# Five plain transposes for both halves of a value column, and partition sums in three column tiles

## The chip, the cores and the metric

The kernel runs on one core of one Trainium2 chip. The metric is the device time of one execution in microseconds (us); lower is better. TensorE (PE) multiplies; its weight loads are listed apart as PEld. VectorE (DVE), ScalarE (ACT) and GpSimd (POOL) do elementwise work, and SyncE (SP) issues nearly all DMAs, in order, from one queue.

## The reference

Two layers of a decoder trunk on 512 prompt tokens and 64 sample tokens (8 sequences of 8), all in float32:

```
h = x + 0.5 * rmsnorm(swiglu(rmsnorm(x)))            # ff1: 1024 -> 2816 -> 1024
z = rmsnorm(h) @ w_in                                # 3584 columns: aq|ak|av|bq|bf|bi|bg
a = dilated window attention(aq, ak, av)             # 8 heads of 64; the samples also read 2048 cached rows
b = HGRN2(q=silu(bq), f=lb+(1-lb)*sigmoid(bf), i=bi) # 4 heads of 128, chunkwise recurrence
b = rmsnorm(b) * silu(bg)
h = h + rmsnorm([rmsnorm(a), b] @ w_out)
h = h + 0.5 * rmsnorm(swiglu(rmsnorm(h)))            # ff2
```

It returns the trunk's output, the new keys and values of both groups of tokens, and the HGRN2 states.

## The kernel before, in words

Tokens lie along the free dimension. They are cut into two halves (hf 0 and 1) of 288: 256 prompt tokens and 32 sample tokens each. Features lie on the 128 partitions. Every weight tile of 128 rows by 128 columns is split into a high and a low part (L114 on ACT, L116 on DVE), and each product is three matmuls (L357 to L359) of 128x288. PE's rows of these three lines are called products below; 24 of them make one output column block of one half.

A layer runs ff1, the input projection with both mixers beside it (`mixing`), w_out, and ff2. In `mixing`, column block i runs for half 0 and then for half 1. Blocks 0 to 7 are queries and keys, blocks 8 to 11 the attention values, blocks 12 to 23 the HGRN2 columns of four heads (every third of them a value column), 24 to 27 the gates. Between products the kernel pulls steps of side work: the samples' attention (`sample`: scores `sc` L860, transposes of the weights `ptps` L895, weighted sums `pov` L915), the prompt's attention (`psc`, `ptp`, `ppv`) and the HGRN2 heads (`lev`, `kv`, `po`). A scheduler in the tile framework then sets the final order on each engine from the program and from its own estimate of times.

Three pieces matter here.

- `tok_major` (L505 to L512) turns a value column to token-major form. For each half it makes two plain transposes of 128 tokens (L508), and for the 32 samples a matmul with the identity (L509) that sits in one 32-column tile of the array (`tile_position=(0, 32*hf)`). Two ACT copies move the result out of PSUM. There are 8 value columns in a layer, so 16 halves. The evacuated column `z` (L525) comes from a ring of six shared temporaries, and for blocks 8 to 11 a DMA per half writes it to `o_v` (L532).
- `stats` (L200 to L217) sums squares over the partitions: three matmuls `stat` (L204) with 96 tokens as stationary columns and a column of ones moving. DVE (L206) and POOL (L207) make the inverse root, and three transposes `bc` (L212) spread it over the partitions. A float32 matmul that is not a transpose appears in the trace as two passes, so the 3 appear as 6.
- `kv_load` (L817 to L830) streams the cached keys and values in tiles of 256 KB through a ring of KVB = 9 buffers. The load into a buffer waits until PE has used the tile that was there; it stands in SP's one queue with the weight loads and the writes.

The PSUM tiles of the products (`mm`) in blocks 4 to 27 come from a pool of two: a new block may start only when the block two before it has been evacuated.

Of the kernel before, what the change touches and what calls it, by code (L numbers as in the profile page):

```python
# [19 lines left out]
P = 128  # L20
D = 1024
NJ = 8
NF = 22
CHUNKS = ((0, 8), (8, 15), (15, 22))
H = 288
HP = 256
# [5 lines left out]
XBUF = 5  # L32
ZBUF = 2
ABUF = 2
KVB = 9
G_OFF = {}
_o = 0
for _n, _w in (("ff1_pre_g", 8), ("ff1_post_g", 8), ("mix_pre_g", 8), ("attn_norm_g", 4), ("hgrn_norm_g", 1),
# [9 lines left out]
def trunk_step(ctx: ExitStack, tc: tile.TileContext, a, L):  # L48
    nc = tc.nc

    pe, act, dve, pool, sp = nc.tensor, nc.scalar, nc.vector, nc.gpsimd, nc.sync
# [4 lines left out]
    cp = ctx.enter_context(tc.tile_pool(name="consts", bufs=1))  # L56
# [85 lines left out]
    logit = const("logits", [P, L, 4])  # L142
    ones = cp.tile([P, 1], F32, name="ones")
    dve.memset(ones[:], 1.0)
    warm = cp.tile([P, 1], F32, name="warm")
# [14 lines left out]
    lbm = cp.tile([P, 4], F32, name="lbm")  # L160
    lbe = cp.tile([P, L, 4], F32, name="lbe")
    lbs = cp.tile([P, 4], F32, name="lbs")
# [4 lines left out]
    def late_consts():  # L167
        lstage = tmp("lstage")[:, :NLM * 32].rearrange("p (a b) -> p a b", b=32)
        for n, t in (("logits", logit), ("lmask", lstage), ("pbias", pbias), ("sb_str", sb_str), ("sb_rec", sb_rec),
                     ("sb_new", sb_new), ("bmask", bmask), ("eye32", eye32), ("sel", sel)):  # L170
            sp.dma_start(t if n == "lmask" else t[:], a[n])
        dve.tensor_copy(lmask[:], lstage)

        dve.tensor_copy(lbm[:], logit[:, 0, :])
        for l in range(1, L):
            dve.tensor_tensor(lbm[:], lbm[:], logit[:, l, :], op=ALU.max)
        for l in range(L):
            dve.tensor_tensor(lbe[:, l, :], logit[:, l, :], lbm[:], op=ALU.subtract)
        act.activation(lbe[:], lbe[:], AF.Exp)
        dve.tensor_copy(lbs[:], lbe[:, 0, :])  # L180
        for l in range(1, L):
            dve.tensor_tensor(lbs[:], lbs[:], lbe[:, l, :], op=ALU.add)
        dve.reciprocal(lbs[:], lbs[:])
        for l in range(L):
            dve.tensor_tensor(lbe[:, l, :], lbe[:, l, :], lbs[:], op=ALU.mult)
        dve.tensor_copy(lbm[:], lbe[:, 0, :])
        for l in range(L):
            if l:
                dve.tensor_tensor(lbm[:], lbm[:], lbe[:, l, :], op=ALU.add)
            dve.tensor_tensor(fof[:, l, :], lbm[:], lbe[:, 0, :], op=ALU.subtract)  # L190
            dve.tensor_scalar(fsc[:, l, :], fof[:, l, :], -0.5, 0.5, op0=ALU.mult, op1=ALU.add)
            dve.tensor_scalar(nfs[:, l, :], fsc[:, l, :], -1.0, None, op0=ALU.mult)
            dve.tensor_tensor(fof[:, l, :], fof[:, l, :], fsc[:, l, :], op=ALU.add)


    def tmp(name="tmp"):
        return tp.tile([P, H], F32, name=name, tag="tmp", bufs=6)


    def stats(acc, inv, out_psum=False, tag="rb"):  # L200

        s = ps_hg.tile([P, 512], F32, name="stat", tag="hg")
        for c in range(3):
            pe.matmul(s[:96, c:c + 1], acc[:, 96 * c:96 * c + 96], ones[:, 0:1], start=True, stop=True)  # L204
        sm = tp.tile([96, 4], F32, name="sm", tag="sm", bufs=2)
        dve.tensor_scalar(sm[:, :3], s[:96, :3], inv, EPS, op0=ALU.mult, op1=ALU.add)  # L206
        pool.tensor_tensor(sm[:, :3], sm[:, :3], nhalf[:96, :3], op=ALU.pow)  # L207
        yield
        yield
        b = ps_hg.tile([P, 512], F32, name="bc", tag="hg")  # L210
        for c in range(3):
            pe.transpose(b[:, 96 * c:96 * c + 96], sm[:, c:c + 1].to_broadcast([96, P]), ident[:96, :96])  # L212
        if out_psum:
            return b[:, :H]
# [122 lines left out]
    late = []  # L337
# [134 lines left out]
    def mixing(l, chains, xpool_close, x_spill):  # L472
        o = [None, None]
        with ExitStack() as es:
# [7 lines left out]
            z = {}  # L482
# [19 lines left out]
                    z[name, h] = pools["hp"].tile([P, 2, H], F32, name=name, bufs=ZBUF)  # L502
                return z[name, h]

            def tok_major(src, hf, dst, dst_s, cols):  # L505
                ps = ps_pr.tile([P, 512], F32, name="tr", tag="pr")
                for q in range(2):
                    pe.transpose(ps[:, q * P:(q + 1) * P], src[:, q * P:(q + 1) * P], ident[:])  # L508
                pe.matmul(ps[32 * hf:32 * hf + 32, 2 * P:3 * P], src[:, HP:H], ident[:], start=True, stop=True,  # L509
                          tile_position=(0, 32 * hf))  # L510
                act.activation(dst[:, 2 * hf:2 * hf + 2, cols], ps[:, :HP].rearrange("p (a b) -> p a b", a=2), AF.Copy)
                act.activation(dst_s[32 * hf:32 * hf + 32, cols], ps[32 * hf:32 * hf + 32, 2 * P:3 * P], AF.Copy)  # L512

            def evac(i, hf, pst):
                ps = pst[:, :H]
                r = rn[hf]
                if i < 8:
                    dst = (aq if i < 4 else ak)[:, i % 4, hf, :]
                    dve.tensor_tensor(dst, ps, r, op=ALU.mult)
                    if i == 7 and hf == 1:  # L520
                        late.append(lambda: sp.dma_start(a["o_k"][l], ak[:]))
                    return
                t = tmp("z")
                if i < 12 or (i < 24 and i % 3 == 2):
                    dve.tensor_tensor(t[:], ps, r, op=ALU.mult)  # L525
                else:
                    dve.scalar_tensor_tensor(t[:], ps, 0.5, r, op0=ALU.mult, op1=ALU.mult)
                    th = tmp("th")
                    act.activation(th[:], t[:], AF.Tanh)
                if i < 12:  # L530
                    m = i - 8
                    sp.dma_start(a["o_v"][l, :, m, hf, :], t[:])  # L532
                    late.append(lambda: tok_major(t, hf, vt, vts, slice(m * P, (m + 1) * P)))
                    return
                h, kind = divmod(i - 12, 3) if i < 24 else (i - 24, 3)
                if hf == 0 and kind < 3 and h >= 2:
                    while stage[h - 2] < kind + 1:
                        drain()
                if kind == 0:
                    dve.tensor_scalar(zt("zf", h)[:, hf, :], th[:], fsc[:, l, h:h + 1], fof[:, l, h:h + 1],  # L540
                                      op0=ALU.mult, op1=ALU.add)
                    pool.tensor_scalar(zt("zk", h)[:, hf, :], th[:], nfs[:, l, h:h + 1], fsc[:, l, h:h + 1],
                                       op0=ALU.mult, op1=ALU.add)
                elif kind == 1:
                    dve.scalar_tensor_tensor(zt("zq", h)[:, hf, :], th[:], 1.0, t[:], op0=ALU.add, op1=ALU.mult)
                elif kind == 2:
                    if ("vh", h) not in z:
                        z["vh", h] = pools["hp"].tile([P, 4, P], F32, name="vh", bufs=ZBUF)
                        z["vhs", h] = pools["hp"].tile([64, P], F32, name="vhs", bufs=ZBUF)
                    late.append(lambda: tok_major(t, hf, z["vh", h], z["vhs", h], slice(0, P)))  # L550
# [636 lines left out]


def _outs(L):
    return {"o_y": (2, P, NJ, H), "o_k": (L, P, 4, 2, H), "o_v": (L, P, 4, 2, H), "o_sp": (L, 4, P, P),  # L1190
            "o_ss": (L, 4, P, NB, P)}


def _unpack(r, L):
    y = np.transpose(r["o_y"], (0, 3, 2, 1)).reshape(2, H, D)
    yp = np.ascontiguousarray(y[:, :HP]).reshape(1, 2 * HP, D)
    ys = np.ascontiguousarray(y[:, HP:]).reshape(NB, 8, D)

    def kv(t):
        t = np.transpose(t, (0, 3, 4, 2, 1)).reshape(L, 2, H, 8, 64)  # L1200
        return (np.ascontiguousarray(t[:, :, :HP]).reshape(L, 1, 2 * HP, 8, 64),
                np.ascontiguousarray(t[:, :, HP:]).reshape(L, NB, 8, 8, 64))

    kp, ks = kv(r["o_k"])
    vp, vs = kv(r["o_v"])
# [22 lines left out]
```

## Time and profile before

| what | value |
|---|---|
| median of 3 runs | 2571.57 us (2571.02 to 2574.45) |
| the profiled execution | 2571.23 us, of which the span from first to last instruction 2569.4 us |
| PE busy | 2523.4 us, 98% of the span |
| DVE, ACT, POOL busy | 1183.7, 903.5, 380.4 us |
| granted clock | 0.997 of full speed |

PE is busy nearly all of the time. Its matmuls are pipelined: the trace gives each a duration of some 0.29 us, but the next one starts about 0.13 us later. What a piece of side work costs is therefore read from starts: how much later the next products start than they would have.

### The profile page before, as it was taken

The page shows a single profiled execution, that of the slowest core. Times are in us where ns is not written, and L with a number is a line of the kernel's source. Part 1 is how long each engine was busy: PE and PEld are TensorE (multiplying, and loading weights), DVE is VectorE, ACT ScalarE, POOL GpSimd, SP SyncE. Part 2 cuts the span into 40 slices and gives each one's busy share as a digit, 9 for nine tenths or more (in the row PEclk, how much of TensorE's full clock was granted, in tenths as well). Part 3 has the DMA queues.
Part 4 walks back from the last instruction along what each step waited for, and adds up shares of the span by engine and source line. Part 5 has one row for each costly group of instructions (what it writes and reads, how often), then busy time and mean ns, then how long its engine had stood idle before and what let it go on. Part 6 is the DMA issues. An engine that isn't in the chain of part 4 may idle for free.

```text
span 2569.4 us, 52156 instructions
## 1 busy us (share of the span) xinstructions
PE 2523.4 (98%) x21876; PEld 2384.3 (93%) x21876; DVE 1183.7 (46%) x2648; ACT 903.5 (35%) x2031; POOL 380.4 (15%) x450
## 2 busy tenths in 40 slices
PE   8999999999999999999999999999999999999997
PEld 8999999877778999999999999998777799999997
DVE  6324335435655742433463334362456557323343
ACT  5222235133335532222542222351333354322232
POOL 1101012002312210101220010120022122101013
PEclk9999999999999999999999999999999999999999
DMA  5222222475543322222222222235754442222221
GB/s 173 83 84 81 91 76 92 169 255 176 187 166 109 100 83 84 82 89 78 88 75 83 83 82 88 77 104 182 253 198 151 155 131 81 86 85 75 91 76 45
DMA packets 108747, 292.04 MB, mean 114 GB/s; under 512 B 12896, under 2 KB 16224, under 8 KB 107744
## 3 DMA queue, kind: packets, MB, share of 16 engines
q1 hardware_dynamic: 108080, 288.29, 34.9%
q8 instruction: 172, 2.82, 0.5%
q14 instruction: 63, 0.52, 0.1%
q10 hardware_dynamic: 432, 0.41, 0.0%
HBM read 272.14 MB, written 16.52 MB: 112 GB/s over the span
## 4 chain that ended last, share of the span: by engine, by line
PE 91%; DVE 4%; issue 2%; POOL 1%; ACT 1%; DMA 0%; SPq 0%; POOLq 0%; ACTq 0%; DVEq 0%
PE gu L358 14%; PE gu L359 14%; PE gu L357 14%; PE mm L357 12%; PE mm L358 12%; PE mm L359 12%; PE sc L860 2%; PE pov L915 1%; PE ppv L800 1%; PE psc L776 1%; POOL sm L207 1%; PE stat L204 1%; PE ptp L791 1%; DVE y L317 1%; PE wo L358 1%
## 5 line engine op out<-in xcount | busy, mean ns | idle before, releaser
L357 PE MATMUL gu<-xh,whi 128*128 128x288 f32 x2752 | 811.6, 295 | 7.4 <-ACT xh L271 6.5
L358 PE MATMUL gu<-xl,whi 128*128 128x288 f32 x2752 | 813.4, 296 | 0.3
L359 PE MATMUL gu<-xh,wlo 128*128 128x288 f32 x2752 | 811.6, 295 | 0.0
L114 ACT ACTIVATE whi<-wraw 128x512 fp32r<-128x512 f32 (+1 forms) x688 | 395.0, 615 | 723.2 <-PE gu L358 357.3
L116 DVE TENSOR_TENSOR wlo<-wraw,whi 128x512 fp32r<-128x512 f32 (+1 forms) x688 | 445.9, 680 | 206.6 <-ACT whi L114 188.6
L357 PEld LDWEIGHTS gu<-xh,whi 128*128 128x128 f32 x2752 | 518.4, 188 | 8.7 <-ACT xh L271 6.9
L358 PEld LDWEIGHTS gu<-xl,whi 128*128 128x128 f32 x2752 | 518.4, 188 | 1.6 <-DVE xl L272 1.6
L359 PEld LDWEIGHTS gu<-xh,wlo 128*128 128x128 f32 x2752 | 518.5, 188 | 0.0
L358 PE MATMUL mm<-hl,whi 128*128 128x288 f32 x1408 | 415.6, 295 | 0.0
L357 PE MATMUL mm<-hh,whi 128*128 128x288 f32 x1408 | 415.0, 295 | 0.0
L359 PE MATMUL mm<-hh,wlo 128*128 128x288 f32 x1408 | 414.6, 294 | 0.0
L438 POOL TENSOR_TENSOR gate<-gate,rb 128x288 f32<-128x288 f32 x176 | 162.9, 925 | 1261.9 <-ACT gate L437 1261.9
L357 PE MATMUL mm<-xh,whi 128*128 128x288 f32 x1088 | 333.9, 307 | 0.7 <-DVE y L453 0.7
L358 PE MATMUL mm<-xl,whi 128*128 128x288 f32 x1088 | 325.7, 299 | 0.0
L359 PE MATMUL mm<-xh,wlo 128*128 128x288 f32 x1088 | 325.0, 299 | 0.0
L359 PEld LDWEIGHTS mm<-hh,wlo 128*128 128x128 f32 x1408 | 264.7, 188 | 0.0
L357 PEld LDWEIGHTS mm<-hh,whi 128*128 128x128 f32 x1408 | 264.6, 188 | 0.0
L358 PEld LDWEIGHTS mm<-hl,whi 128*128 128x128 f32 x1408 | 264.4, 188 | 0.0
L442 DVE TENSOR_TENSOR hid<-gu,gate 128x288 f32<-128x288 f32 x172 | 78.7, 457 | 329.2 <-PE gu L359 320.9
L357 PEld LDWEIGHTS mm<-xh,whi 128*128 128x128 f32 x1088 | 204.4, 188 | 21.1 <-issue 17.6
L358 PEld LDWEIGHTS mm<-xl,whi 128*128 128x128 f32 x1088 | 204.9, 188 | 10.0 <-issue 9.1
L359 PEld LDWEIGHTS mm<-xh,wlo 128*128 128x128 f32 x1088 | 204.9, 188 | 6.8 <-issue 6.6
(196 smaller groups left out, 2373.3 us busy)
## 6 DMA issues: line engine op xcount, KB each, us to landing
wraw<-in_wgu SPq DMA_DIRECT2D x175, 512.0 KB, 3.5
kv<-in_kc SPq DMA_DIRECT2D x160, 256.0 KB, 4.1
kv<-in_vc SPq DMA_DIRECT2D x160, 256.0 KB, 3.9
wraw<-in_wd SPq DMA_DIRECT2D x64, 448.0 KB, 3.3
wraw<-in_w_in SPq DMA_DIRECT2D x56, 512.0 KB, 4.2
wraw<-in_wd SPq DMA_DIRECT2D x32, 512.0 KB, 3.5
wraw<-in_w_out SPq DMA_DIRECT2D x16, 512.0 KB, 4.2
xs<-x SPq DMA_DIRECT2D x4, 1152.0 KB, 4.4
```

Source lines behind the costliest of these rows:

```text
L114: act.activation(whi[i][:, c], r[:, c], AF.Copy)
L116: dve.tensor_tensor(wlo[i][:, c], r[:, c], f(whi[i][:, c]), op=ALU.subtract)
L204: pe.matmul(s[:96, c:c + 1], acc[:, 96 * c:96 * c + 96], ones[:, 0:1], start=True, stop=True)
L207: pool.tensor_tensor(sm[:, :3], sm[:, :3], nhalf[:96, :3], op=ALU.pow)
L317: ins = dve.tensor_tensor(y[:, js, :], y[:, js, :], rb[:, None, :].to_broadcast([P, 2, H]), op=ALU.mult)
L357: pe.matmul(ps, wh[:, s], xhi[:, j, :], start=(n == 0), stop=False)
L358: pe.matmul(ps, wh[:, s], xlo[:, j, :], start=False, stop=False)
L359: pe.matmul(ps, wl[:, s], xhi[:, j, :], start=False, stop=(n == k - 1))
L438: pool.tensor_tensor(g[:], g[:], rn[hf], op=ALU.mult)
L442: dve.tensor_tensor(h[:], ps, gate[hf][:], op=ALU.mult)
L776: pe.matmul(dst, q, kk, start=True, stop=True, tile_position=(64 * s, 0))
L860: pe.matmul(ps[32 * p:32 * p + 32, c], qbd[:, 2 * bp + bb, p, :], rhs(p), start=(bb == 0), stop=(bb == 1), tile_position=(0, 32 * p))
```

## The change

`tok_major` now runs once for a value column, when both halves are evacuated into one tile `zt` of 576 columns. Half 1 is stored with its samples next to those of half 0 (two DVE operations in place of one), so that the turn is four plain transposes of 128 tokens and a fifth of 64 tokens, into two PSUM tiles, with two ACT copies. `zt` has one buffer. The write of `o_v` is one DMA for both halves, and the host puts the columns back in order. `stats` makes nine matmuls of 32 stationary columns, one in each of three column tiles for each of three token groups, in place of three of 96. KVB falls from 9 to 8. The constants behind the lower bounds (`logits` and what is worked out of them) move into a temporary tile.

```
-KVB = 9
+KVB = 8
...
         s = ps_hg.tile([P, 512], F32, name="stat", tag="hg")
         for c in range(3):
-            pe.matmul(s[:96, c:c + 1], acc[:, 96 * c:96 * c + 96], ones[:, 0:1], start=True, stop=True)
+            for q in range(3):
+                pe.matmul(s[32 * q:32 * q + 32, c:c + 1], acc[:, 96 * c + 32 * q:96 * c + 32 * q + 32], ones[:, 0:1],
+                          start=True, stop=True, tile_position=(0, 32 * q))
...
-            def tok_major(src, hf, dst, dst_s, cols):
+            def tok_major(src, dst, dst_s, cols):
                 ps = ps_pr.tile([P, 512], F32, name="tr", tag="pr")
-                for q in range(2):
-                    pe.transpose(ps[:, q * P:(q + 1) * P], src[:, q * P:(q + 1) * P], ident[:])
-                pe.matmul(ps[32 * hf:32 * hf + 32, 2 * P:3 * P], src[:, HP:H], ident[:], start=True, stop=True,
-                          tile_position=(0, 32 * hf))
-                act.activation(dst[:, 2 * hf:2 * hf + 2, cols], ps[:, :HP].rearrange("p (a b) -> p a b", a=2), AF.Copy)
-                act.activation(dst_s[32 * hf:32 * hf + 32, cols], ps[32 * hf:32 * hf + 32, 2 * P:3 * P], AF.Copy)
+                for c in range(4):
+                    o_ = c * P + 64 * (c // 2)
+                    pe.transpose(ps[:, c * P:(c + 1) * P], src[:, o_:o_ + P], ident[:])
+                pn = ps_pr.tile([P, 512], F32, name="trs", tag="pr")
+                pe.transpose(pn[:64, :P], src[:, HP:HP + 64], ident[:])
+                act.activation(dst[:, :, cols], ps[:].rearrange("p (a b) -> p a b", a=4), AF.Copy)
+                act.activation(dst_s[:, cols], pn[:64, :P], AF.Copy)
...
-                t = tmp("z")
                 if i < 12 or (i < 24 and i % 3 == 2):
-                    dve.tensor_tensor(t[:], ps, r, op=ALU.mult)
+                    if hf == 0:
+                        z["t"] = qp.tile([P, 2 * H], F32, name="zt")
+                    t2 = z["t"]
+                    if hf == 0:
+                        dve.tensor_tensor(t2[:, :H], ps, r, op=ALU.mult)
+                    else:
+                        dve.tensor_tensor(t2[:, H + 32:], ps[:, :HP], r[:, :HP], op=ALU.mult)
+                        dve.tensor_tensor(t2[:, H:H + 32], ps[:, HP:], r[:, HP:], op=ALU.mult)
...
-                    sp.dma_start(a["o_v"][l, :, m, hf, :], t[:])
-                    late.append(lambda: tok_major(t, hf, vt, vts, slice(m * P, (m + 1) * P)))
+                    if hf:
+                        sp.dma_start(a["o_v"][l, :, m], t2[:])
+                        late.append(lambda: tok_major(t2, vt, vts, slice(m * P, (m + 1) * P)))
```

The scheduler moves instructions on every engine. Three places show what the prediction speaks of. The first is on PE, in `mixing` of layer 0, where a sum (`stat`) of an HGRN2 head stands between the samples' `pov` and the next head's `lev`, both of which are in 32-column tiles. Before:

```order
L359 MATMUL mm<-xh_4545,wlo 128x288
L915 MATMUL pov<-kv,pts 32x128 x16
L204 MATMUL stat<-ones,osq 96x1 x3
L594 MATMUL lev<-zq,zk 32x32 x16
L791 MATMUL ptp<-ident,S 128x128 x7
L594 MATMUL lev<-zq,zk 32x32 x16
```

and now:

```order
L361 MATMUL mm<-xh_4560,wlo 128x288
L927 MATMUL pov<-kv,pts 32x128 x16
L205 MATMUL stat<-ones,osq 32x1 x9
L606 MATMUL lev<-zq,zk 32x32 x16
L803 MATMUL ptp<-ident,S 128x128 x4
L606 MATMUL lev<-zq,zk 32x32 x8
```

The sum keeps its place, but it is in column tiles like its neighbours.

The second is on PE at the attention values of layer 0, around the transposes `ptps` and the first sums `pov` of the samples. Before, products stand between `ptps` and `pov`, and the turn of one half (`tr`) lies around `pov`:

```order
L895 MATMUL ptps<-ident,ss 128x128 x2
L895 MATMUL ptps<-ident,ss 64x128
L357 MATMUL mm<-xh_4545,whi 128x288
L358 MATMUL mm<-xl_4546,whi 128x288
L359 MATMUL mm<-xh_4545,wlo 128x288
L508 MATMUL tr<-ident,z 128x128
L915 MATMUL pov<-kv,pts 32x128 x36
L508 MATMUL tr<-ident,z 128x128
L509 MATMUL tr<-ident,z 32x128
L357 MATMUL mm<-xh_4735,whi 128x288
```

Now `ptps` and `pov` follow each other at once, at the boundary between two blocks:

```order
L361 MATMUL mm<-xh_4756,wlo 128x288
L907 MATMUL ptps<-ident,ss 128x128 x10
L907 MATMUL ptps<-ident,ss 64x128
L927 MATMUL pov<-kv,pts 32x128 x32
L359 MATMUL mm<-xh_4560,whi 128x288
```

No product is left between them, and the turn of a whole value column stands one block later, in five plain transposes (`tr` x4 and `trs`):

```order
L360 MATMUL mm<-xl_4757,whi 128x288
L361 MATMUL mm<-xh_4756,wlo 128x288
L511 MATMUL tr<-ident,zt 128x128 x4
L513 MATMUL trs<-ident,zt 64x128
L927 MATMUL pov<-kv,pts 32x128 x4
```

The third is SP's queue from the end of the keys to the third attention value of layer 0; `kv` are the cache loads, `out_o_v` the writes of the values. Before:

```order
L521 DMA out_o_k<-ak 128x2304
L532 DMA out_o_v<-z 128x288
L826 DMA kv<-in_kc 128x512 x14
L532 DMA out_o_v<-z 128x288
L826 DMA kv<-in_kc 128x512 x6
L829 DMA kv<-in_vc 128x512 x2
L532 DMA out_o_v<-z 128x288
L829 DMA kv<-in_vc 128x512 x6
```

and now:

```order
L524 DMA out_o_k<-ak 128x2304
L838 DMA kv<-in_kc 128x512 x13
L543 DMA out_o_v<-zt 128x576
L838 DMA kv<-in_kc 128x512 x7
L841 DMA kv<-in_vc 128x512 x7
L543 DMA out_o_v<-zt 128x576
L841 DMA kv<-in_vc 128x512
```

The write of a whole column now stands behind 13 and then 14 cache loads, and the next evacuation into `zt` waits for that write.

## Rows read from the trace of the kernel before

**Rows 1.** The page: the chain that ended last, by engine
```profile
PE 91%; DVE 4%; issue 2%; POOL 1%; ACT 1%; DMA 0%; SPq 0%; POOLq 0%; ACTq 0%; DVEq 0%
```
**Rows 2.** Busy us by stretch: window, length, PE, PEld, DVE, ACT, POOL; clock, DMA, GB/s
```profile
496.60:546.90 50.30, 50.30 (x447) 34.58 (x447) 13.27 (x43) 13.96 (x36) 1.76 (x5) 1.00 0.78 252
546.90:805.80 258.90, 249.22 (x3231) 198.83 (x3231) 148.26 (x467) 97.19 (x275) 56.77 (x80) 0.99 0.53 177
```
**Rows 3.** Timeline of PE (start, us, line): one half's turn between products
```profile
495.82 0.29 PE L359 MATMUL mm<-xh,wlo 128*128 128x288 f32 x1
495.95 0.38 PE L508 MATMUL tr<-ident,z 128*128 128x128 f32 x2
496.26 0.41 PE L509 MATMUL tr<-ident,z 128*32 128x128 f32 x2
...
496.83 0.29 PE L358 MATMUL mm<-xl,whi 128*128 128x288 f32 x1
```
**Rows 4.** Timeline of PE: eight plain transposes between products
```profile
528.92 0.29 PE L359 MATMUL mm<-xh,wlo 128*128 128x288 f32 x1
529.06 1.04 PE L895 MATMUL ptps<-ident,ss 128*128 128x128 f32 x8
...
530.07 0.29 PE L358 MATMUL mm<-xl,whi 128*128 128x288 f32 x1
```
**Rows 5.** Timeline of PE: one sum of six 96-column passes between products
```profile
446.37 0.29 PE L359 MATMUL mm<-xh,wlo 128*128 128x288 f32 x1
446.51 0.59 PE L204 MATMUL stat<-ones,y 128*96 128x1 f32 x6
446.96 0.38 PE L357 MATMUL mm<-xh,whi 128*128 128x288 f32 x1
447.17 0.29 PE L358 MATMUL mm<-xl,whi 128*128 128x288 f32 x1
```
**Rows 6.** Timeline of PE: 32-column passes in four column tiles, in and out
```profile
586.65 0.29 PE L357 MATMUL mm<-xh,whi 128*128 128x288 f32 x1
586.88 0.46 PE L594 MATMUL lev<-zq,zk 128*32 128x32 f32 x32
587.15 0.26 PE L598 MATMUL lev<-zq,zk 128*32 128x32 f32 x4
...
594.09 0.26 PE L598 MATMUL lev<-zq,zk 128*32 128x32 f32 x4
594.27 0.40 PE L357 MATMUL mm<-xh,whi 128*128 128x288 f32 x1
594.51 0.29 PE L358 MATMUL mm<-xl,whi 128*128 128x288 f32 x1
```
**Rows 7.** Timeline of PE: a sum between two runs in column tiles
```profile
701.01 0.67 PE L204 MATMUL stat<-ones,osq 128*96 128x1 f32 x6
701.61 0.46 PE L594 MATMUL lev<-zq,zk 128*32 128x32 f32 x32
```
**Rows 8.** Timeline of DVE: second halves of the first and second value evacuated
```profile
496.14 0.46 DVE L525 TENSOR_TENSOR z<-mm,rb 128x288 f32<-128x288 f32 x1 [2.71 <-PE mm L359]
...
510.02 0.46 DVE L525 TENSOR_TENSOR z<-mm,rb 128x288 f32<-128x288 f32 x1 [0.28 <-PE mm L359]
```
**Rows 9.** Timeline of SP: the cache loads, and the write behind them
```profile
496.14 9.52 SPq L826 DMA_DIRECT2D kv<-in_kc  x14
505.75 0.38 SPq L532 DMA_DIRECT2D out_o_v<-z  x1
```
**Rows 10.** DMA issues: median us from issue to landing, the values' writes
```profile
out_o_v<-z SPq DMA_DIRECT2D x16, 144.0 KB, 3.9
```
**Rows 11.** Timeline of PE, then ACT: the last `ptps`, and its last copy
```profile
530.35 0.55 PE L895 MATMUL ptps<-ident,ss 128*128 128x128 f32 x3
...
531.21 0.26 ACT L903 ACTIVATE pts<-ptps 64x128 f32<-64x128 f32 x1
```
**Rows 12.** Groups by shape: weight loads of `pov`, idle before them
```profile
L915 PEld LDWEIGHTS pov<-kv,pts 128*32 128x32 f32 x1280 | 32.9, 109 | 6.6 <-issue 5.8 <-PE mm L358 0.4 <-DMA kv<-in_vc 0.2
```

More of the change, by code (lines that the diff above doesn't have):

```diff
@@ L141, in trunk_step @@
     sel = const("sel", [P, 32])
-    logit = const("logits", [P, L, 4])
     ones = cp.tile([P, 1], F32, name="ones")
@@ L158, in trunk_step @@
             dve.tensor_scalar(g_of(l, n), g_of(l, n), 0.5, None, op0=ALU.mult)
-    lbm = cp.tile([P, 4], F32, name="lbm")
-    lbe = cp.tile([P, L, 4], F32, name="lbe")
-    lbs = cp.tile([P, 4], F32, name="lbs")
     fsc = cp.tile([P, L, 4], F32, name="fsc")
@@ L167, in late_consts @@
     def late_consts():
+        lb = tmp("lb")
+        logit = lb[:, :4 * L].rearrange("p (a b) -> p a b", b=4)
+        lbe = lb[:, 4 * L:8 * L].rearrange("p (a b) -> p a b", b=4)
+        lbm, lbs = lb[:, 8 * L:8 * L + 4], lb[:, 8 * L + 4:8 * L + 8]
         lstage = tmp("lstage")[:, :NLM * 32].rearrange("p (a b) -> p a b", b=32)
@@ L170, in late_consts @@
                      ("sb_new", sb_new), ("bmask", bmask), ("eye32", eye32), ("sel", sel)):
-            sp.dma_start(t if n == "lmask" else t[:], a[n])
+            sp.dma_start(t if n in ("lmask", "logits") else t[:], a[n])
         dve.tensor_copy(lmask[:], lstage)
-        dve.tensor_copy(lbm[:], logit[:, 0, :])
+        dve.tensor_copy(lbm, logit[:, 0, :])
         for l in range(1, L):
-            dve.tensor_tensor(lbm[:], lbm[:], logit[:, l, :], op=ALU.max)
+            dve.tensor_tensor(lbm, lbm, logit[:, l, :], op=ALU.max)
         for l in range(L):
-            dve.tensor_tensor(lbe[:, l, :], logit[:, l, :], lbm[:], op=ALU.subtract)
-        act.activation(lbe[:], lbe[:], AF.Exp)
-        dve.tensor_copy(lbs[:], lbe[:, 0, :])
+            dve.tensor_tensor(lbe[:, l, :], logit[:, l, :], lbm, op=ALU.subtract)
+        act.activation(lbe, lbe, AF.Exp)
+        dve.tensor_copy(lbs, lbe[:, 0, :])
         for l in range(1, L):
-            dve.tensor_tensor(lbs[:], lbs[:], lbe[:, l, :], op=ALU.add)
-        dve.reciprocal(lbs[:], lbs[:])
+            dve.tensor_tensor(lbs, lbs, lbe[:, l, :], op=ALU.add)
+        dve.reciprocal(lbs, lbs)
         for l in range(L):
-            dve.tensor_tensor(lbe[:, l, :], lbe[:, l, :], lbs[:], op=ALU.mult)
-        dve.tensor_copy(lbm[:], lbe[:, 0, :])
+            dve.tensor_tensor(lbe[:, l, :], lbe[:, l, :], lbs, op=ALU.mult)
+        dve.tensor_copy(lbm, lbe[:, 0, :])
         for l in range(L):
             if l:
-                dve.tensor_tensor(lbm[:], lbm[:], lbe[:, l, :], op=ALU.add)
-            dve.tensor_tensor(fof[:, l, :], lbm[:], lbe[:, 0, :], op=ALU.subtract)
+                dve.tensor_tensor(lbm, lbm, lbe[:, l, :], op=ALU.add)
+            dve.tensor_tensor(fof[:, l, :], lbm, lbe[:, 0, :], op=ALU.subtract)
             dve.tensor_scalar(fsc[:, l, :], fof[:, l, :], -0.5, 0.5, op0=ALU.mult, op1=ALU.add)
@@ L522, in evac @@
                     return
-                t = tmp("z")
                 if i < 12 or (i < 24 and i % 3 == 2):
-                    dve.tensor_tensor(t[:], ps, r, op=ALU.mult)
+                    if hf == 0:
[6 more added lines that the diff above has]
+                        dve.tensor_tensor(t2[:, H:H + 32], ps[:, HP:], r[:, HP:], op=ALU.mult)
                 else:
+                    t = tmp("z")
                     dve.scalar_tensor_tensor(t[:], ps, 0.5, r, op0=ALU.mult, op1=ALU.mult)
@@ L549, in evac @@
                         z["vhs", h] = pools["hp"].tile([64, P], F32, name="vhs", bufs=ZBUF)
-                    late.append(lambda: tok_major(t, hf, z["vh", h], z["vhs", h], slice(0, P)))
+                    if hf:
+                        late.append(lambda: tok_major(t2, z["vh", h], z["vhs", h], slice(0, P)))
                 else:
@@ L1189, in _outs @@
 def _outs(L):
-    return {"o_y": (2, P, NJ, H), "o_k": (L, P, 4, 2, H), "o_v": (L, P, 4, 2, H), "o_sp": (L, 4, P, P),
+    return {"o_y": (2, P, NJ, H), "o_k": (L, P, 4, 2, H), "o_v": (L, P, 4, 2 * H), "o_sp": (L, 4, P, P),
             "o_ss": (L, 4, P, NB, P)}
@@ L1204, in _unpack @@
     kp, ks = kv(r["o_k"])
-    vp, vs = kv(r["o_v"])
+    v = r["o_v"]
+    v = np.stack([v[..., :H], np.concatenate([v[..., H + 32:], v[..., H:H + 32]], -1)], -2)
+    vp, vs = kv(v)
     sp = np.ascontiguousarray(r["o_sp"]).reshape(L, 1, 4, P, P)
```

## Prediction, made before the run

> **What bounds the kernel now.** I read the chain of waits first. 91% of it is PE [rows 1]: what ends the kernel is the stream of PE's instructions, so a change is worth what it takes out of that stream, less what PE waits more. Next I read the busy times by stretch. In the stretch of the attention values PE has no gap (50.30 us of 50.30) and the DMA engines are busy 0.78 of it; in the rest of `mixing` PE has 249.22 us of 258.90, so some 10 us a layer are waits [rows 2]. DVE, ACT and POOL are far from full there. Last I read PE's timeline around each piece that the change touches. Durations overlap, so I compare starts: two products in a row start 0.133 us apart, and I call "cost" of a piece the time between the products around it less the product pitches in between.
>
> **The turns.** Between products, one half's turn takes 495.82 to 496.83 with two product pitches in it: 1.01 - 0.27 = 0.74 us [rows 3]. Two plain transposes are 0.22 of it (eight of them cost 530.07 - 528.92 - 0.27 = 0.88 us, 0.11 each, with nothing for going in or out [rows 4]). The other 0.52 us are two passes in a column tile and the way into and out of that tile: the second product after tiled work starts 0.24 us after the first rather than 0.13 [rows 6].
>
> After the change a value column needs five plain transposes: 5 x 0.11 = 0.55 us. In two layers there are 16 columns, 32 halves. If every half stood alone, the gain would be 32 x 0.74 - 16 x 0.55 = 14.9 us. It is less, because most halves share a run with scores or sums that are in column tiles anyway: in the order of before 4 of the 16 halves of a layer stand alone. A shared half costs at least its transposes and a little of the passes beside the neighbours', 0.28 us, so the lower end is 8 x 0.74 + 24 x 0.28 - 8.8 = 3.8 us. I take 0.49 for a shared half, between 0.28 and 0.74, since some halves share one side only: 8 x 0.74 + 24 x 0.49 - 8.8 = 8.9, so -9 us (ends -4 and -15).
>
> **The sums.** There are 44 (132 matmuls of L204 in the order, three each). One alone takes 446.37 to 447.17: 0.80 - 0.27 = 0.53 us, of which the six passes of 96 columns are 0.45 [rows 5]. The trace of before has no pass with one moving column in a 32-column tile. The nearest row is `lev`, 128 rows by 32 columns with 32 moving columns: 32 passes start within 586.88 to 587.15, 0.27 us, four tiles side by side, so 0.034 us for a round of four [rows 6]. Nine matmuls are 18 passes, in three tiles six rounds: 0.20 us. Going in, the first tiled pass starts 0.23 us after the product before it, not 0.13; going out, four passes and the exit took 594.09 to 594.27, 0.18, so about 0.12 for the exit, and then 0.24 to the second product [rows 6]. Alone, a sum after the change costs 0.23 + 0.20 + 0.12 + 0.24 - 0.27 = 0.52 us against 0.53. So where a sum stands between products or plain transposes, nothing is won: the switch into tiles eats what the passes save.
>
> It is won where the neighbours are tiled. By the order that is so on both sides for 6 sums (the first place shown with the change is one) and on one side for 4. On both sides, 701.01 to 701.61 (0.60 us to the next `lev`) [rows 7] becomes 0.20, and the 0.1 to go out of `pov` falls away too: 0.5 to 0.6 each, 3.3 us for six. On one side about 0.3, 1.2 us for four. Two pairs come together into one run of 18 matmuls, which saves two switches of 0.3: 0.6. The remaining ones at 0.02 are 0.7, and the last sum of the kernel, with PE idle around it, is 0.3 sooner. Sum: -6 us. The bounds come from the pass. If the tiles take turns rather than run side by side, a 32-column pass costs a third of a 96-column one, 0.45 / 6 / 3 = 0.025, and 18 of them 0.45: then each of some 38 sums costs 0.25 us more than now and the term is +9. If six rounds hide altogether under the switch, 44 x 0.20 more is won, -15. I take -6, by `lev`, which has the same rows and columns.
>
> The Trainium skill, "TensorEngine Tiling (Array Packing)", section "Performance Considerations", speaks against these nine matmuls: each matmul has an overhead of about 60 cycles on this chip, one moving column takes as long as 60, and a tiling factor should not be taken from a dimension that is already small. At the full clock 60 cycles are 25 ns, an estimate from that page; one after another, 18 passes would be 0.45 us and the term +9. The rows of `lev` start 8 ns apart on average, so the overhead can lie side by side in tiles. The same page's "Key Properties" says that a change of tiling mode drains the array; the rows above show that as 0.23 and 0.24 in place of 0.13.
>
> **The waits that are added.** `zt` has one buffer. The evacuation of half 0 of the next value waits for the turn of the last one, which is on PE right after that product, and for its write to land. The write is issued in SP's queue behind 13 and 14 cache loads (third place shown with the change). In the trace such a queue cost a lot: the first value's second half was evacuated by 496.60 [rows 8], and its write, behind 14 loads from 496.14, was issued at 505.75 [rows 9]; it lands some 3.9 us later [rows 10]. What is queued behind the waiting DVE instruction are the masks of the scores, weight splits and further evacuations; PE waits when the product after next needs the PSUM tile. It has about two blocks of 3.2 us and the side work between them before that. By these rows: the write of the first column is issued at about 505 and landed at 509; before, the block ahead of the one that needs the tile ended on PE at about 509.9 (its evacuation starts at 510.02 [rows 8]), and in the new order scores and no products stand at that boundary. That just fits: 0 to 0.5 us. The second write stands behind loads that wait for the last scores, and there the scheduler put `ptps` and `pov` in a row with no product between them (second place). `pov` waits for the copies: 530.90, the end of the last `ptps`, to 531.47, the end of its last copy, is 0.6 us [rows 11], and with eleven in a row up to 1. So about 1.2 us a layer. With 8 cache buffers each load starts one tile later. PE lost 0.2 us to these loads at `pov` before [rows 12]; I set 1.3 us a layer where `pov` eats tiles faster than they come. Sum +5 us (ends 0 and +27, the latter if each of the six waits on `zt` costs PE a landing and its issue, 4.5 us).
>
> Three things I cost at nothing. The extra DVE operation per column and the fewer ACT copies lie beside PE. The bounds' constants move to a later place in ff1 with the same instructions; a PSUM tile there comes up again only four blocks of 3.2 us later, which covers them, and without that cover it is their chain once, some 3 us. One DMA for two carries the same bytes.
>
> **The sum.** -9 - 6 + 5 = -10 us against the profiled execution of 2571.23: 2561.2. It lies 0.3 under the median of 2571.57, so I say 2561.
>
> **Rivals.**
> - *The waits don't bite.* PE had no gap at the values before [rows 2], and the scheduler has set the order around the new waits. Then 2571.2 - 9 - 6 = 2556; with the turns at their best 2550. Against it: the new order itself leaves PE nothing to do between `ptps` and `pov`.
> - *No change.* What PE no longer does at the HGRN2 heads, it waits: 10 us a layer in `mixing` are waits already [rows 2], and `lev` waits on DVE and POOL whatever PE does between. Then half of -15 goes, and with +5 the time is 2571.2 - 7.5 + 5 = 2569.
> - *Slower by the single buffer.* If the write lands later than PE's slack at all three values of both layers, 2571.2 - 15 + 27 = 2583. It decides from 2.5 us a wait. For it: the 9.6 us that a write sat in the queue. Against it: the loads before it wait for scores that now come earlier in PE's order than the block that needs the tile.
> - *Slower by the tiles.* If column tiles with one moving column take turns, 2571.2 - 9 + 9 + 5 = 2576. It decides from 0.36 us for the 18 passes. Against it: the rows of `lev`.
>
> **How the numbers follow.** This kernel's measurement can tell 0.2%, 5.1 us, from no change. The forecast, 2552 to 2566, has 0.62; the waits that don't bite 0.14; no change 0.15; the single buffer 0.06; the tiles 0.03. So faster 0.76, same 0.15, slower 0.09. The range reaches from 2550, the turns at their best without waits, to 2573: above it lie the two slower cases, below it little.
>
> **What would show it.** In the profile of after: 396 sums' matmuls as 792 passes with starts 7 to 12 ns apart, and 0.2 us from a sum between `pov` and `lev` to `lev`; a sum alone between products still near 0.5 us. Five transposes between products at 0.55 us. In the stretch of the values, PE idle before `pov` of 0.6 to 1 us, and a wait of DVE for `out_o_v` that ends before PE needs the tile. If instead PE idles 2 us or more at a product that follows a value, for a DVE evacuation that waited for a write, the single buffer decided. If passes of a sum start 25 ns apart, the tiles take turns.

## Result and the profile after

The changed kernel takes 2559.16 us (median of 4 runs, 2558.65 to 2561.06) against 2571.61 for the kernel before beside it: 12.4 us less, ratio 0.9948, interval 0.9936 to 0.9959. The forecast was 2561. The profiled execution took 2559.31, its span is 2557.5 (before: 2571.23 and 2569.4).

The chain that ended last, on the page of after; it answers to [rows 1]:

```profile
PE 90%; DVE 6%; ACT 2%; issue 1%; POOL 1%; DMA 0%; SPq 0%; ACTq 0%; POOLq 0%; DVEq 0%
```

PE still sets the end. DVE has gone from 4% to 6% of the chain; these are shares of the work that the chain passes through, not waits, and 27 of the 43 us of difference lie between the two layers' `mixing`, where the time is as before. What PE works and waits, the busy times by stretch say (columns as in [rows 2]: window, length, then busy PE, PEld, DVE, ACT, POOL; clock, DMA, GB/s). Of after, the attention values and the rest of `mixing`, cut at the same products as in [rows 2], in layer 0 and in layer 1:

```profile
492.83:541.52 48.69, 46.74 (x441) 33.54 (x439) 13.49 (x47) 12.24 (x28) 2.20 (x5) 1.00 0.82 273
541.52:797.43 255.91, 243.58 (x3339) 194.40 (x3339) 148.58 (x471) 96.74 (x268) 56.71 (x80) 0.99 0.53 176
1759.88:1808.50 48.62, 46.76 (x441) 33.55 (x439) 13.61 (x47) 12.23 (x28) 2.17 (x6) 1.00 0.84 274
1808.50:2063.51 255.01, 243.19 (x3339) 194.19 (x3337) 148.89 (x472) 96.75 (x268) 56.47 (x80) 1.00 0.54 177
```

The same stretches of layer 1 in before:

```profile
1768.91:1819.30 50.39, 50.39 (x447) 34.63 (x447) 13.40 (x43) 13.96 (x36) 1.75 (x6) 1.00 0.76 250
1819.30:2076.89 257.59, 247.92 (x3230) 197.61 (x3230) 148.40 (x466) 97.17 (x275) 56.79 (x80) 1.00 0.53 177
```

In the values PE works 3.6 us less a layer and waits 1.9 us that it did not wait before: 1.6 to 1.8 us are left. In the rest of layer 1 it works 4.7 us less and waits 11.8 us in place of 9.7: 2.6 us are left, in layer 0 3.0. The two layers together: 3.4 + 5.6 = 9.0 of the 11.9 us between the spans. Another 3.5 us lie ahead of product 168 (31.3 us from the first product before, 27.8 after). They are not all the change's: the kernel below with only a smaller ring, which has the same instructions there as before, took 30.5, and five kernels below that have those of after took 27.7 to 29.6. Between products 48 and 168 these five and after all take 18.5 us, before 19.4; what varies lies ahead of product 48.

The pieces on PE, as rows. A timeline of after (start, us, engine, line), five plain transposes between products:

```profile
572.66 0.29 PE L361 MATMUL mm<-xh,wlo 128*128 128x288 f32 x1
572.78 0.62 PE L511 MATMUL tr<-ident,zt 128*128 128x128 f32 x4
573.24 0.27 PE L513 MATMUL trs<-ident,zt 128*64 128x128 f32 x1
573.27 0.38 PE L359 MATMUL mm<-xh,whi 128*128 128x288 f32 x1
573.48 0.30 PE L360 MATMUL mm<-xl,whi 128*128 128x288 f32 x1
```

573.48 - 572.66 - 0.27 = 0.55 us for both halves, where one half took 0.74 [rows 3]. A sum alone between products:

```profile
437.65 0.29 PE L361 MATMUL mm<-xh,wlo 128*128 128x288 f32 x1
437.87 0.36 PE L205 MATMUL stat<-ones,acc 128*32 128x1 f32 x18
438.16 0.40 PE L359 MATMUL mm<-xh,whi 128*128 128x288 f32 x1
438.40 0.29 PE L360 MATMUL mm<-xl,whi 128*128 128x288 f32 x1
```

438.40 - 437.65 - 0.27 = 0.48 us, where it took 0.53 [rows 5]. And a sum between two tiled runs, where it took 0.60 to the next `lev` [rows 7]:

```profile
694.34 0.31 PE L205 MATMUL stat<-ones,osq 128*32 128x1 f32 x15
694.48 0.22 PE L606 MATMUL lev<-zq,zk 128*32 128x32 f32 x1
```

Here it takes 0.14 us to the first `lev` (three more passes lie between the levels behind it). So each piece takes on PE about what its working said. What the time shows of it is another matter, and the experiments are about that.

### The profile page after: what moved, and what is told of

The parts are those of the page before. It is cut to its first block, busy times and chain, and to the rows that moved or that the text cites. A ratio compares the mean times of both kernels' runs of the same rounds, so it can differ in the third digit from the quotient of the medians.

```text
span 2557.5 us, 53049 instructions
## 1 busy us (share of the span) xinstructions
PE 2503.5 (98%) x22356; PEld 2369.7 (93%) x22356; DVE 1180.9 (46%) x2664; ACT 897.8 (35%) x1999; POOL 378.6 (15%) x450
## 4 chain that ended last, share of the span: by engine, by line
PE 90%; DVE 6%; ACT 2%; issue 1%; POOL 1%; DMA 0%; SPq 0%; ACTq 0%; POOLq 0%; DVEq 0%
PE gu L360 14%; PE gu L359 14%; PE gu L361 14%; PE mm L359 12%; PE mm L361 12%; PE mm L360 12%; PE sc L872 1%; PE ppv L812 1%; PE pov L927 1%; PE ptp L803 1%; DVE xl L274 1%; DVE x L322 1%; DVE y L319 1%; PE psc L788 1%; DVE wlo L116 1%
```

## Experiments

Each kernel was timed in five rounds beside the kernel before. "Below before" is the difference of the two medians taken side by side (before: 2572.43, then 2572.15, then 2572.74); in brackets stands the interval of the ratio. The changed kernel itself stands 12.4 below its own neighbour. Where a kernel is compared with the changed one, this can be read from the two medians or from what each has below before; the two readings differ by up to 1.2 us.

**The sums alone** (before, with this edit only):

```diff
-            pe.matmul(s[:96, c:c + 1], acc[:, 96 * c:96 * c + 96], ones[:, 0:1], start=True, stop=True)
+            for q in range(3):
+                pe.matmul(s[32 * q:32 * q + 32, c:c + 1], acc[:, 96 * c + 32 * q:96 * c + 32 * q + 32], ones[:, 0:1],
+                          start=True, stop=True, tile_position=(0, 32 * q))
```

> The kernel before with one edit, the nine sums in three column tiles. Theory (18 passes run side by side, 0.2 us; gain only where neighbours are tiled): -6 us against the kernel before, 2565.6; a sum alone between products 0.49 to 0.52 us against 0.53, starts of its passes 7 to 12 ns apart. Rival 'half is waited again': -3 us, 2568.5, with the waits of PE on DVE and POOL in the heads up by 3 us. Rival 'tiles take turns': +9 us, 2580, passes 25 ns apart.

2569.1, 3.3 below before; ratio 0.9991 (0.9983 to 1.0), which is 2.3 us, with an interval that reaches no change. About half of the -6 that I had predicted, so nearer the rival's number. But the median lies between two groups. The mean granted clock is listed for each execution: six at 0.996 or 0.997 took 2567.1 to 2569.1 us, five at 0.994 or 0.995 took 2571.1 to 2573.8. The six have a median of 2567.8, executions of before at 0.996 or more 2572.1: by these the sums are worth some 4 us. Its rest of `mixing`:

```profile
544.63:801.32 256.69, 245.08 (x3351) 194.84 (x3350) 148.12 (x467) 97.92 (x276) 56.87 (x80) 1.00 0.53 177
1815.26:2073.32 258.06, 246.47 (x3350) 195.96 (x3350) 148.24 (x467) 97.89 (x276) 56.86 (x80) 0.99 0.53 176
```

A stretch at half the clock (told of at the end) adds 1.7 us to the second row, and one as long to the row of layer 0 of before [rows 2]. Without these two, PE works 2.4 and 3.2 us less than before, and the stretches are 0.5 and 1.2 us shorter: 1.7 won of 5.6. The other 3.9 us are longer waits, as the rival said.

**The turns, the constants and the ring of 8, with the old sums** (after, with the edit above undone):

> The changed kernel with the sums as they were before (three matmuls of 96 columns): the turns, the constants' move and 8 cache buffers remain. Theory (turns -9, waits +5, and what the constants and the start bring): -4 to -7 us, 2565 to 2567.5; in the stretch of the attention values 1.5 to 2 us less than before in each layer. Rival 'the waits eat the turns': -1 to -3 us, 2569 to 2571, and the stretch of the values as long as before.

2564.76, 7.7 below before; ratio 0.9973 (0.9964 to 0.9983). The turns carry most of the gain, and with the sums' 3.3 the parts make 11.0 of the 12.4. Its values and rest of `mixing`, in layer 0 and in layer 1:

```profile
494.50:544.22 49.72, 46.83 (x440) 33.58 (x439) 13.60 (x47) 12.23 (x28) 2.17 (x5) 1.00 0.81 267
544.22:799.56 255.34, 245.33 (x3218) 196.45 (x3218) 148.93 (x471) 96.65 (x268) 56.78 (x80) 1.00 0.54 178
1764.13:1812.81 48.68, 46.76 (x441) 33.55 (x439) 13.61 (x47) 12.23 (x28) 2.17 (x5) 1.00 0.83 273
1812.81:2067.81 255.00, 244.58 (x3218) 195.90 (x3218) 148.82 (x470) 96.03 (x267) 56.75 (x80) 1.00 0.54 177
```

With the stretches at half the clock taken out (1.7 us in before, 0.7 here), PE works 13.3 us less in these four than before and waits 5.9 us more, so they are 7.4 us shorter. The values gain 1.7 us in layer 1, as expected, but only 0.6 in layer 0, where one wait for the samples' queries (`sc` for `qbd`) is 1.0 us long.

**The heads' sums plain again** (after; 16 sums of 44):

```diff
         for c in range(3):
+            if out_psum:
+                pe.matmul(s[:96, c:c + 1], acc[:, 96 * c:96 * c + 96], ones[:, 0:1], start=True, stop=True)
+                continue
             for q in range(3):
```

> The changed kernel with the sums of the HGRN2 heads (16 of 44) plain again, three matmuls of 96 columns, and the other 28 in tiles. By the prediction's working the heads are where the tiles gain (0.57 us each where both neighbours are tiled, 0.3 on one side, 0.6 for a pair): +5 to +6, about 2564.5. Rival, from the run of the sums alone (-2.3 in place of -6): most of what the heads' sums save is given back in pauses of TensorE right behind, or in one more stretch at half the clock: +0 to +2, about 2560.

2560.53, 12.2 below before (0.9943 to 0.9968): 1.4 above the changed kernel by its own median, 0.2 counted from before. So the rival holds: the heads' tiles win nearly nothing. Its rest of `mixing`, to be read beside the second and fourth row of after:

```profile
543.60:798.85 255.25, 245.34 (x3243) 195.81 (x3242) 149.21 (x471) 96.06 (x267) 56.57 (x80) 1.00 0.53 175
1809.99:2064.96 254.97, 245.24 (x3243) 196.61 (x3242) 149.51 (x472) 96.75 (x268) 56.81 (x80) 1.00 0.54 178
```

With tiled sums at the heads PE works 1.8 and 2.1 us less (243.58 and 243.19), and the stretches are 0.7 longer and the same (255.91 and 255.01). Stretches at half the clock account for 1.7 us of after's layer 0, 1.0 of its layer 1 and 1.1 of this kernel's layer 1. Without them PE works 5.4 us less over both layers, and 0.9 us of it is won. The rest is waits. From the list of PE's waits in that stretch of layer 0, for after:

```profile
PE lev L606 <- DVE zq L655: 1.5, 2, 0.8
PE lev L606 <- DVE zq L675: 1.2, 1, 1.2
PE lev L606 <- POOL zk L677: 1.1, 1, 1.1
...
PE bc L214 <- POOL sm L209: 0.9, 2, 0.5
...
PE sc L872 <- DMA kv<-in_kc: 0.6, 1, 0.6
```

and for this kernel (its lines are 3 higher):

```profile
PE lev L609 <- DVE zq L658: 1.3, 2, 0.8
...
PE lev L609 <- POOL zk L680: 1.0, 3, 0.5
...
PE sc L875 <- DMA kv<-in_kc: 0.4, 1, 0.4
```

After waits longer in several places. The two largest differences are 1.2 us at a `lev` for a decay product (`zq` L675) and 0.9 us at `bc` for the second step of a sum (`sm` on POOL, which it takes from DVE); this kernel has no such rows. PE comes sooner to work that DVE, POOL and the loads have not yet got ready.

The other 28 sums are another matter. They are the difference between this kernel (12.2 below) and the one with the turns alone (7.7 below): 4.5 us, where the working had about 1, and where 0.05 us each by the row of a sum alone (0.53 before, 0.48 after) would be 1.4. The intervals of the two ratios overlap, so how much of the 4.5 is theirs stays open.

**Every sum's passes twice** (after):

```diff
-            for q in range(3):
+            for q in (0, 1, 2, 0, 1, 2):
```

> The changed kernel with each of the nine matmuls of a sum issued twice, to the same place: 792 more passes in the tiles, no other change. One sum's 18 passes take 0.19 us in the trace from first to last start, 0.206 with the next pitch. If time taken out of TensorE's stream is time of the kernel everywhere: 44 x 0.206 = +9, about 2568. If at the heads it only takes the place of pauses: the 28 other sums, +5.8, about 2565. If passes lie under the switch of modes: under +2.

2569.5 (2565.56 to 2571.54), 3.2 below before: 10.3 above the changed kernel by medians and 9.2 counted from before, which is the full price. The profiled execution was the quickest of the 11, 6.3 above after's, and in its rest of `mixing` the doubled passes added nothing in layer 0 and at most 1.2 in layer 1 (0.7 of that is a longer stretch at half the clock):

```profile
543.13:798.97 255.84, 244.27 (x3519) 195.79 (x3519) 148.06 (x471) 96.78 (x268) 57.13 (x80) 0.99 0.53 176
1812.58:2068.80 256.22, 244.51 (x3519) 196.04 (x3519) 148.03 (x471) 96.76 (x268) 56.97 (x80) 0.99 0.53 176
```

So some 5 of the 6.3 us lie outside these stretches: there a sum costs what it takes on PE (a sum alone became 0.20 us longer; 5.8 were expected for the 28). At the heads this profile says little is paid and the median says all of it. Six of the 11 executions have a granted clock of 0.994 or 0.995, the profiled one 0.996, so part of the median can be the clock: open.

**The passes tile by tile** (after, only the order of the nine):

```diff
-        for c in range(3):
-            for q in range(3):
+        for q in range(3):
+            for c in range(3):
```

> The changed kernel with the passes of each sum in another order: the three column blocks of one tile one after the other, then the next tile, where the changed kernel goes from tile to tile at every instruction. 396 instructions, 792 passes, the same tiles, the same data. Theory: the passes run as they do in the changed kernel (6 to 7 ns apart, 11 on average) because neighbours lie in different tiles. Then two passes in three now have their neighbour in the same tile, and if such a pass takes the 34 ns of a round of four level passes instead of 11, 528 x 0.023 = 12 us are added: about 2571. Rival: a pass of one column into a tile of 32 columns is short whatever stands beside it, and the order is worth nothing: within 2 us of the changed kernel's 2559. The pitch of the passes decides: over 20 ns by the theory, 6 to 12 by the rival.

2564.08, 8.1 below before (0.9958 to 0.9982), so 4.4 to 4.9 above the changed kernel: between the two numbers. The starts of the 18 passes of one sum, differences in ns read from the two traces:

```
after         7  7 39  7  6 19  6  7 18  7  7 18  7  6 19  6  7   (mean of all 11)
tile by tile 53 31  6 26 27  5 26  5  1 26 27  5 26  5 27 32 31   (mean of all 20)
```

The trace does not name the tile of a pass. But the starts of both lines can be sorted into three chains of six, one for each tile, and then all six chains are the same within 1 ns: 0, 53, 84, 116, 148 and 180 ns from the chain's own first start. In the changed kernel the second and third chain begin 7 and 14 ns after the first, tile by tile 90 and 179 ns after it. By this sorting passes inside a tile start 31 to 32 ns apart from the second on, in either order, near the 34 ns of a round of `lev` [rows 6], and the tiles run side by side; what the order of issue sets is how early the next tile begins. The 18 passes take 193 ns from first to last start in the changed kernel and 359 ns tile by tile, and 44 sums make 7.3 us of that, of which the time shows 4 to 5.

The Trainium skill, "TensorEngine Tiling (Array Packing)", "Performance Considerations", has an overhead of about 60 cycles for a matmul, by an estimate 25 ns at the full clock. By the sorting above the trace shows somewhat more inside one tile, 31 to 32 ns; but where the passes are issued from tile to tile, as in this change, the next tile's pass starts 6 or 7 ns after the one before.

**The single buffer `zt`, and the ring.** Two buffers for `zt` need room, so there is a control, the changed kernel with 4 scratch buffers, and this beside it:

```diff
-        return tp.tile([P, H], F32, name=name, tag="tmp", bufs=6)
+        return tp.tile([P, H], F32, name=name, tag="tmp", bufs=4)
...
-                        z["t"] = qp.tile([P, 2 * H], F32, name="zt")
+                        z["t"] = qp.tile([P, 2 * H], F32, name="zt", bufs=2)
```

> The changed kernel with 4 scratch buffers of a half's width instead of 6: the control for the two kernels beside it, which need the room. If scratch buffers are never what is waited for, 0 (2559); each us above that is to be taken off the other two. My estimate is +1, between 0 and +4.

> The changed kernel with two buffers for the joined values (zt) instead of one, and 4 scratch buffers, to be read against the control with 4 scratch buffers. By the prediction the single buffer costs 1.2 us a layer: 2.4 us less than the control. Rival: the wait that the changed kernel's trace shows (VectorE idle 6.8 us for the store of the values at 531.72) stands behind products that TensorE has anyway, and no idle time of TensorE ends with it: 0 against the control, within 1 us. A third way: the order written with the second buffer differs in the value stages, and moves the time by 2 us either way without a wait; then the pauses of TensorE there, not VectorE's, tell.

Control 2566.84, two buffers 2567.45: nothing won, as the rival said. The scratch buffers cost 7.7, which I had put at 1. The values of layer 0, of the control and with two buffers:

```profile
493.00:541.65 48.65, 46.73 (x440) 33.51 (x439) 13.48 (x47) 12.24 (x28) 2.20 (x5) 1.00 0.82 274
493.09:542.82 49.73, 48.84 (x440) 34.10 (x439) 13.66 (x47) 12.36 (x28) 2.20 (x5) 1.00 0.78 254
```

With two buffers PE waits 1.0 us less but works 2.1 us more: the scheduler wrote another order, so this run alone does not show that the single buffer is free. What shows it for the changed kernel is its list of waits, further down. With the ring of 9, again beside the control:

```diff
-KVB = 8
+KVB = 9
```

> The changed kernel with the ring of key and value buffers back at 9 instead of 8, and 4 scratch buffers, to be read against the control with 4 scratch buffers. By the prediction the smaller ring costs 1.3 us a layer: 2.6 us less than the control. In the order of before the same step from 9 to 8 cost 7.6 us: if that holds in the new order too, 7 to 8 us less than the control, and if the control costs no more than 1, this kernel is the fastest of all at about 2552. Rival: with the turns taken together the ring is drained at other times and its size no longer shows: 0 against the control.

2564.49, 2.3 below the control, which looks like the 2.6 predicted. The profiles do not bear it out: the values of this kernel are 0.3 us longer than the control's, and the spans (2559.9 and 2564.2) differ by less than three stretches at half the clock that only the control has. This profiled execution was the quickest of its six, so for the medians it stays open. With a ring of 7, on the changed kernel as it is:

```diff
-KVB = 8
+KVB = 7
```

> The changed kernel with a ring of 7 key and value buffers instead of 8, nothing else. From 9 to 8 cost 2.3 us in the new order (with 4 scratch buffers) and 7.6 us in the old one. Theory: each load starts one tile later and PE waits for it where pov or sc eats tiles faster than they come, so 7 costs at least as much again: +2 to +6, about 2563, and more idle time of PE that ends with the loads. Rival: the ring's size only shuffles the order and the loads are early enough: within 1 us of 2559.

2570.31, 2.4 below before: 10 to 11 above the changed kernel, beyond the theory's range. Now the waits are there. PE's waits in its values, and below them the two longest in the rest of layer 0:

```profile
PE mm L359 <- DVE zt L531: 1.7, 1, 1.7
PE ptps L907 <- ACT pts L913: 0.4, 1, 0.4
PE ptps L907 <- ACT ss L898: 0.4, 1, 0.4
PE sc L872 <- DVE qbd L853: 0.3, 1, 0.3
...
PE sc L872 <- DMA kv<-in_kc: 2.9, 4, 1.2
PE lev L606 <- DVE zq L655: 1.5, 2, 0.8
```

The same list for the values of the changed kernel, and two rows of its DVE:

```profile
PE scn L872 <- DVE smx L867: 0.8, 1, 0.8
PE ptps L907 <- ACT pts L913: 0.4, 1, 0.4
PE ptps L907 <- ACT ss L898: 0.4, 1, 0.4
PE sc L872 <- DVE qbd L853: 0.3, 1, 0.3
```

```profile
524.73 0.18 DVE L534 TENSOR_TENSOR zt<-mm,rb 128x32 f32<-128x32 f32 x1
531.72 0.46 DVE L531 TENSOR_TENSOR zt<-mm,rb 128x288 f32<-128x288 f32 x1 [6.81 <-DMA out_o_v<-zt]
```

So DVE does wait 6.8 us for the write of the values, and no wait of PE ends with it. With a ring of 7, the write comes so late that the product behind it waits 1.7 us: the mechanism of the single buffer is real. It does not simply grow as the ring shrinks: with a ring of 9 and 4 scratch buffers the same product waits 0.8 us in each layer. Nor are these waits all that the ring of 7 costs. In its profile the values and the rest of `mixing` of both layers are 13.3 us longer than after's at the same clock: 6.9 us more waits, and 6.4 us more work of PE in another order.

**Two parts by themselves in the old order.** Before with only the constants' move, and before with only the smaller ring:

```diff
-    logit = const("logits", [P, L, 4])
...
+        lb = tmp("lb")
```

```diff
-KVB = 9
+KVB = 8
```

> The kernel before with the constants behind the lower bounds moved into a temporary tile, nothing else. In the two profiles, the changed kernel is 3.2 us ahead at 37 us, before any turn. Theory 'the move does it': -3 us, 2568.5, ahead by 3 at 37 us. Rival 'the first 2.3 us come from when the first loads land and the clock rises, which differs from run to run': -1 us, 2570.6, ahead by about 0.9 at 37 us once the start of product 48 is taken out.

> The kernel before with 8 cache buffers in place of 9. Prediction's term: +1.3 us a layer, +2.6, 2574.2, as PE idle before pov at the attention values. Rival 'the order is set around it': 0, 2571.6.

2574.76 (ratio 1.0 to 1.0018) and 2580.06 (1.0019 to 1.0044): 2.3 and 7.6 above before. For the constants both theory and rival had a gain; the ring costs three times its 2.6. Yet all parts together are 12.4 below. The constants' kernel is ahead at the start, as the theory said (28.7 us from the first product to product 168, before 31.3), but its values and rest of `mixing` are 4.1 us longer at the same clock. With the smaller ring those stretches are 7.9 us longer, 2.1 of it waits and 5.8 more work of PE in another order. So it is not shown that 8 buffers are too few in the old order; most of the loss is the order that the scheduler writes for them. And the reverse of the constants' move on the changed kernel (they are written over `fsc` and `nfs` before these hold their own values):

```diff
-        lb = tmp("lb")
-        logit = lb[:, :4 * L].rearrange("p (a b) -> p a b", b=4)
...
+        logit, lbe = fsc[:], lbt[:]
+        lbm, lbs = nfs[:, 1, :], nfs[:, 0, :]
```

> The changed kernel with the constants of the bounds in tiles of their own again (written over fsc and nfs before these hold their own values, for lack of room) instead of in a scratch buffer, so that the ring of scratch buffers stands where it stood before. Theory: the scratch buffer that the changed kernel takes there costs what it cost alone in the old order, 2.3 us: 2557. Rival: the move costs nothing by itself, and the 2.3 us were another order of the mixing stages with other pauses: then this kernel lies anywhere from 3 us below to 5 us above 2559, and its trace differs from the changed kernel's in the mixing stages and not at the start.

2558.38 (2556.85 to 2562.49), ratio 0.9948 (0.9936 to 0.9961) as for the changed kernel: 0.8 below it by its own median, which these runs can't tell from nothing. It is the lowest median here, and no version is clearly faster than the changed kernel.

## Why the prediction was right, and where it was not

The time came out 1.8 us below the forecast. The direction and the main term are right, but that the sum came so close is in part luck: the turns with their waits brought 3.7 us more than forecast, the sums 1.3 to 2.7 less.

- *The turns* (-9). Five transposes take the forecast 0.55 us. Turns, ring and constants together gave -7.7, where the forecast for them, with its waits, was -4. By stretches before and after, that kernel's gain lies in the values and the rest of `mixing`, as said. The term was too small: PE works 13.3 us less there, inside the range of 4 to 15 that was given.
- *The sums* (-6). The step that failed is "it is won where the neighbours are tiled", 3.3 + 1.2 + 0.6. The pieces were right: 0.14 and 0.48 us in the rows, for 0.20 and 0.52 forecast. But 5.1 us out of PE's stream at the heads are not 5.1 us of the kernel. PE's work fell by 5.4 us, the time of these stretches by 0.9. "Nothing is won" elsewhere was too low: by the row of one sum the other 28 win 0.05 us each, 1.4 by an estimate, and by the medians up to 4.5. Measured, the sums alone: -3.3, beside the turns -4.7. At the heads this is the rival "no change", at the place it named, but for the heads' sums and not for the turns.
- *The bounds of the pass*. The tiles run side by side (18 passes in 0.19 us, for 0.20 forecast); the worse bound (+9) did not come; the order of issue that the change has keeps off 4 to 5 us of it.
- *The waits that are added* (+5). Before the sums come in, the waits grew by 5.9 us, so the size was right; in the values PE waits 1.9 us a layer, in part for other things than I said. No wait of PE ends with `zt` (forecast 0 to 0.5 us a layer). The wait that I expected at `pov` (0.6 to 1 us) stands one step earlier, 0.4 + 0.4 us at `ptps`, and another 0.8 at `scn` for a maximum was not foreseen. The ring of 8 (forecast 1.3 us a layer) shows no wait in the values that ends with a load, and one of 0.6 us behind them; a ring of 7 costs 10 to 11 us more.
- *Nothing for the constants.* Not settled: 2.3 us in the old order, 0.8 by the medians in the new one, with intervals that overlap.
- *Ahead of product 168* I forecast nothing but a few hundredths for the sums; 3.5 us of the difference of the two profiled executions lie there; 0.9 of it is the same in every kernel with these instructions, and up to 1.9 us vary among executions of the same instructions, by chance.

## To carry to other kernels

Time taken out of the bounding engine is not yet time of the kernel. In a stretch that already has waits on several other engines, ask first how much of the saving each of them will let through: for the heads' sums it was a sixth to a third. Even in the values, where PE had no gap before, 3.6 us less work gave 1.6 to 1.8. Small passes in column tiles are cheap if the order of issue goes from tile to tile, and that order is as much a part of such a change as the tiles. A ring one smaller cost PE a wait of some 0.6 us a layer in one order and the kernel 8 to 11 us in others, and half of that or more was a new order rather than a wait; so try such sizes in the order in which they will stand.

## What the runs showed that I had not expected

TensorE's granted clock falls to 0.5, its level of 1.2 GHz, for 3.4 us at a time, once or twice in most of the profiled executions. By an estimate each stretch costs about 1.7 us (half of 3.4 us, where PE is busy throughout; products start 0.24 us apart in it and 0.133 outside), as much as a term of the sum. Busy times by stretch, of the changed kernel and of the control with 4 scratch buffers, ahead of a fall and in it:

```profile
624.60:628.00 3.40, 2.50 (x65) 1.42 (x61) 3.40 (x14) 0.38 (x1) 0.04 (x1) 1.00 0.96 319
628.00:631.40 3.40, 3.40 (x48) 2.40 (x48) 1.97 (x10) 0.20 (x1) 1.77 (x2) 0.50 1.03 377
```

```profile
1943.00:1946.50 3.50, 2.67 (x68) 1.58 (x64) 2.23 (x5) 0.46 (x1) 0.00 (x0) 1.00 0.04 15
1946.50:1953.30 6.80, 6.80 (x65) 5.30 (x64) 4.01 (x11) 0.72 (x3) 1.78 (x2) 0.50 0.41 149
```

In the rows ahead of the two falls PE had waited 0.9 and 0.8 us. Beside the tail, before has one such stretch, after two, the control three (two in a row), and the kernels with a ring of 9 and with the constants back have none. So part of what differs by 2 to 5 us between these kernels can be how often the clock falls; the two groups of the sums alone lie 5 us apart. No run here took the falls away alone, so what share they have in the medians stays open.
